# Start of a two-layer mixer trunk: squares folded on VectorE, the first modulation group taken k tile by k tile, lambda moved behind the conditioning row

## The chip, the cores and the metric

The kernel runs on one core of a Trainium2 chip, as one program. The metric is the device time of one execution in microseconds; the time of a kernel is the median of its runs. TensorE, VectorE, ScalarE and GpSimd each work through their own instruction queue in order, SyncE issues nearly all the transfers.

## The reference

256 tokens of width 2048 (16 tiles of 128 features) go through two layers. Each layer normalises the residual stream, modulates it with a scale and a shift made from a conditioning vector c, projects it once into the inputs of three mixers, and projects their gated outputs back.

```python
c_act = jax.nn.silu(c)
for l in range(DEPTH):
    shift, scale, gate = jnp.split(c_act @ w_ada[l] + b_ada[l], 3, axis=-1)
    h = rms_norm(x, norm_w[l]) * (1.0 + scale[:, None, :]) + shift[:, None, :]
    (gq, gk, gv, glr, gz, dq, dk, dv, da, db, dz, aq, ak, av, az) = jnp.split(h @ w_in[l], bounds, axis=-1)
    ...  # gated linear attention, gated DeltaNet
    lam = jnp.exp(jnp.sum(lv[0] * lv[1])) - jnp.exp(jnp.sum(lv[2] * lv[3])) + lam_init
    ...  # differential attention with lam
    y = jnp.concatenate([o_gla, o_gdn, o_diff], axis=-1) @ w_out[l]
    x = x + gate[:, None, :] * y
```

All is float32. `w_ada` is 2048 x 6144 and `w_in` about 2048 x 8200 for each layer, so the kernel streams some 270 MB of weights.

## The kernel before

The stream is kept with features on the partitions: `xt` is [128, 16 k tiles, 256 tokens]. A float32 product is made of three faster ones: `weights()` (L292) loads a chunk of 128 x 1024 into one of six buffers `raw`, ScalarE rounds it to `wh` (L300), VectorE takes the rest `wl = raw - wh` (L301), and TensorE sums wh·hh, wl·hh and wh·hl, where `hh` and `hl` are the same two parts of the modulated input. `wh` and `wl` have three buffers each.

The modulation's matrix-vector product is done on VectorE. `w_ada` comes in groups of eight pieces of 128 x 1024 (four output tiles, two halves of the sum each); `ada_group` (L313) multiplies each piece with the conditioning row `c_row` and accumulates (L325), and after the eighth piece four short ScalarE sums (L337) close scale and shift of two k tiles. Group g of the first eight gives scale (pieces 0 to 3) and shift (pieces 4 to 7) of k tiles 2g and 2g+1. All but the first group share the six buffers with the weights of the projection.

A layer's projection goes in passes over k, `STEPS` (L68): in layer 0 first blocks 18 to 27 (512 columns each, tokens on the output's partitions) over k tiles 0 and 1, then the same blocks over k tiles 2 and 3, and so on, so that it can start when one group of the modulation is there. Partial results are evacuated and added (`evac`, L427). While a pass runs, `advance` (L1087) traces the products of later groups and the modulation of k tiles between the chunks. Inside one block the order on TensorE is that of the trace, and a scheduler with a simulated timeline and priorities (`tc.high_priority`) writes the order of each engine's queue; `tc.manual_schedule` (`in_order`, L233) fixes the traced order for the engines that it names.

The start: SyncE loads the parameters `pt`, the conditioning row `c16`, the identity (first part of `ct`), x in four parts, and the first group's eight pieces `fr`. ScalarE squares x by parts, GpSimd folds the squares (L1066, L1068). In `rstd_rows` (L361) TensorE sums the squares over the partitions, GpSimd takes the power -1/2, ScalarE scales the identity by it twice (`dg`, L378), TensorE spreads it over the partitions, ScalarE copies that to `rb` in SBUF. `modulate` (L383) makes hn = rb · scale · x on VectorE (L388), `hh` on ScalarE (L389) and `hl` on VectorE (L390), for two k tiles in a call. The lambda of the differential attention is made at the very start (L272 to L282).

Of the kernel before, what the change touches and what calls it, by code (L numbers as in the profile page):

```python
# [18 lines left out]
P = 128  # L19
# [56 lines left out]
def in_chunks(layer, i):  # L76

    b0, b1, k0, k1 = STEPS[layer][i]
    out = []
    for b in range(b0, b1):  # L80
        for k in range(k0, k1):
            c = out[-1] if out else None
            if c is None or BLOCKS[c[-1][0]][0] != BLOCKS[b][0] or (k == k0 and BLOCKS[b][0] == "T") \
                    or _chunk_elems(c) + _width(b) > RAW:
                out.append([(b, k, k + 1)])
            elif c[-1][0] == b:
                c[-1] = (b, c[-1][1], k + 1)
            else:
                c.append((b, k, k + 1))
    return out  # L90
# [50 lines left out]
def hybrid_trunk(ctx: ExitStack, tc: tile.TileContext, x, cvec, pos, par, w_ada, w_in, w_out, w_lr, qkn, adt, cst, out):  # L141
# [91 lines left out]
    in_order = lambda: tc.manual_schedule(engines={mybir.EngineType.PE})  # L233
# [12 lines left out]
    SP.dma_start(ct[:, 0:128], cst[:, 0:128])  # L246
# [3 lines left out]
    first_raws = []  # L250
# [19 lines left out]
    nlam = const.tile([P, L], F32, name="nlam")  # L270
    ACT.activation(c16, c16, AF.Silu)
    pr = tiny("lp", 2 * L)  # L272
    lam = pcol("lam", 0, 4 * L).rearrange("p (m two) -> p m two", two=2)
    DVE.tensor_tensor(pr.rearrange("p (m o) -> p m o", o=1), lam[:, :, 0:1], lam[:, :, 1:2], ALU.mult)
    pb = bank("lam_ps", "a")
    mm(pb[:, 0:2 * L], ones, pr)
    el = tiny("el", 2 * L)
    ACT.activation(el, pb[:, 0:2 * L], AF.Exp)
    for l in range(L):
        init = 0.8 - 0.6 * math.exp(-0.3 * l)  # L280
        DVE.scalar_tensor_tensor(nlam[:, l:l + 1], el[:, 2 * l + 1:2 * l + 2], -init, el[:, 2 * l:2 * l + 1],
                                 ALU.add, ALU.subtract)  # L282
    for i in range(4):
        cb = bank("c_ps", "p")
        for j in range(4):
            mm(cb[:, 128 * j:128 * j + 128], ident[0:KT, 4 * i + j:4 * i + j + 1].broadcast_to([KT, P]), c16)
        (ACT.copy if i % 2 else DVE.tensor_copy)(c_row[:, 512 * i:512 * i + 512], cb)


    state = {"n": 0}  # L290

    def weights(src, n):  # L292

        raw = wraw.tile([P, RAW], F32, name="raw", tag="raw")[:, 0:n]
        wh = wsp.tile([P, RAW], F32R, name="wh", tag="wh")[:, 0:n]
        wl = wsp.tile([P, RAW], F32R, name="wl", tag="wl")[:, 0:n]
        with tc.high_priority(offset=AHEAD if state["n"] else 0):
            SP.dma_start(raw, src)
# [3 lines left out]
        state["n"] += 1  # L302
        return wh, wl

# [3 lines left out]
    DVE.tensor_scalar(pcol("b_ada", 0, 48 * L), pcol("b_ada", 0, 48 * L), 0.5, None, ALU.mult)  # L308
# [4 lines left out]
    def ada_group(l, g, raws=None):  # L313

        sums = tiny("ada_p", 8)
        for i in range(8):
            if raws is None:
                raw = wraw.tile([P, RAW], F32, name="rawa", tag="raw")[:, 0:1024]
                with tc.high_priority(offset=AHEAD):
                    SP.dma_start(raw, w_ada[l, g, i])  # L320
            else:
                raw = raws[i]
            cb = c_row[:, 1024 * (i % 2):1024 * (i % 2) + 1024]
            with tc.high_priority(offset=AHEAD):
                DVE.scalar_tensor_tensor(raw, raw, 1.0, cb, ALU.mult, ALU.mult, accum_out=sums[:, i:i + 1])  # L325
            if i < 7:
                yield
        for f in range(4):
            if g < 8:
                k = 2 * g + f % 2  # L330
                j = 0 if f < 2 else 1
            else:
                k = 4 * (g - 8) + f
                j = 2
            o, scale = ada[l][:, j, k:k + 1], pcol("norm", 16 * l + k) if j == 0 else 1.0
            bias = pcol("b_ada", 48 * l + (16, 0, 32)[j] + k)
            ACT.activation(tiny("ada_j", 2), sums[:, 2 * f:2 * f + 2], AF.Identity, bias=bias, scale=scale, accum_out=o)  # L337
        yield

    def ada_all():  # L340
        for l in range(L):
            for g in range(12):
                yield from ada_group(l, g, first_raws if l == 0 and g == 0 else None)

    ada_it = ada_all()
    ada_n = [0]
# [14 lines left out]
    def rstd_rows(sqs):  # L361
# [21 lines left out]
    def modulate(l, xt, rb, hh, hl, k):  # L383

        for i in range(k, k + 2):
            h = reg(i % 4, "hn")[:, 0:T]
            scale, shift = ada[l][:, 0, i:i + 1], ada[l][:, 1, i:i + 1]
            DVE.scalar_tensor_tensor(h, rb, scale, xt[:, i, :], ALU.mult, ALU.mult)  # L388
            ACT.activation(hh[:, i, :], h, AF.Identity, bias=shift)  # L389
            DVE.scalar_tensor_tensor(hl[:, i, :], h, shift, hh[:, i, :].bitcast(F32), ALU.add, ALU.subtract)  # L390


    in_off = [0]
# [25 lines left out]
    def project(l, group, hh, hl, o, after):  # L419
# [18 lines left out]
        for chunk in in_chunks(l, group):  # L438
            n = _chunk_elems(chunk)
            src = w_in[in_off[0]:in_off[0] + P * n].rearrange("(p n) -> p n", p=P)  # L440
            in_off[0] += P * n
            wh, wl = weights(src, n)
# [620 lines left out]
    for q in range(4):  # L1063
        p = sqx[:, 4 * q:4 * q + 4, :]
        ACT.activation(p, xt0[:, 4 * q:4 * q + 4, :], AF.Square)
# [6 lines left out]
    ada_to(ada_mark(0, 0))  # L1072

    for l in range(L):
# [12 lines left out]
        def advance(n, l=l, xt=xt, rb=rb, hh=hh, hl=hl, mod=mod):  # L1087

            while True:
                while mod[0] < KT and ada_n[0] >= ada_mark(l, mod[0] // 2):  # L1090
                    with tc.high_priority(offset=AHEAD):
                        modulate(l, xt, rb, hh, hl, mod[0])
# [5 lines left out]
        def block_done(b, done, last, l=l, o=o, g=g):  # L1098
            kind, name, i, _ = BLOCKS[b]
            lo, hi = span  # L1100
            if l == 0 and b == STEPS[0][0][0] and len(seen) == 0:
                seen.add("constants")
                load_constants()
# [55 lines left out]

        for i, (b0, b1, k0, k1) in enumerate(STEPS[l]):  # L1160
            advance(ada_mark(l, (k1 - 1) // 2))
# [126 lines left out]
```

## Time and profile before

| | us |
|---|---|
| median of 3 runs | 1101.14 |
| lowest and highest | 1100.52, 1104.81 |
| profiled execution, its own time | 1103.98 |
| its span, first to last instruction | 1102.2 |

| engine | busy us | share of the span |
|---|---|---|
| TensorE, matmul | 1047.0 | 95% |
| VectorE | 888.6 | 81% |
| ScalarE | 607.2 | 55% |
| GpSimd | 219.8 | 20% |

The profile is of one execution. Times in its rows are from the start of the span. A row of the timeline merges neighbours that are alike: "x8" are eight instructions, the time is from the first one's start to the last one's end. Instructions of one engine overlap a little, so a mean is longer than the distance of two starts. What stands in brackets is the idle time ahead and what ended it. PE is TensorE, PEld its weight loads, DVE VectorE, ACT ScalarE, POOL GpSimd, SP SyncE, and a name with q is the engine's queue of issues.

### The profile page before, as it was taken

The page shows a single profiled execution, that of the slowest core. Times are in us where ns is not written, and L with a number is a line of the kernel's source. Part 1 is how long each engine was busy: PE and PEld are TensorE (multiplying, and loading weights), DVE is VectorE, ACT ScalarE, POOL GpSimd, SP SyncE. Part 2 cuts the span into 40 slices and gives each one's busy share as a digit, 9 for nine tenths or more (in the row PEclk, how much of TensorE's full clock was granted, in tenths as well). Part 3 has the DMA queues.
Part 4 walks back from the last instruction along what each step waited for, and adds up shares of the span by engine and source line. Part 5 has one row for each costly group of instructions (what it writes and reads, how often), then busy time and mean ns, then how long its engine had stood idle before and what let it go on. Part 6 is the DMA issues. An engine that isn't in the chain of part 4 may idle for free.

```text
span 1102.2 us, 19699 instructions
## 1 busy us (share of the span) xinstructions
PE 1047.0 (95%) x7398; PEld 918.9 (83%) x7398; DVE 888.6 (81%) x1365; ACT 607.2 (55%) x1251; POOL 219.8 (20%) x284
## 2 busy tenths in 40 slices
PE   4999999999899989999979999999999999999998
PEld 3768888889898777898977877899989877889998
DVE  5899999998999886888687776677756776787874
ACT  4745544447765646466545555468444556557742
POOL 4000000040130841134210000024222144102400
PEclk9999999999999999999998999999999999999999
DMA  9888999999877545755588888796535645777472
GB/s 352 311 299 308 351 336 341 329 296 339 301 270 254 182 145 188 249 162 186 167 318 327 308 315 319 238 306 228 181 116 174 218 164 172 246 244 236 136 216 90
DMA packets 76799, 273.24 MB, mean 248 GB/s; under 512 B 8816, under 2 KB 9888, under 8 KB 76576
## 3 DMA queue, kind: packets, MB, share of 16 engines
q1 hardware_dynamic: 76704, 271.99, 71.7%
q8 instruction: 58, 0.95, 0.3%
q14 instruction: 37, 0.30, 0.1%
HBM read 267.76 MB, written 4.19 MB: 247 GB/s over the span
## 4 chain that ended last, share of the span: by engine, by line
PE 55%; DVE 18%; DMA 11%; issue 9%; ACT 5%; POOL 2%; SPq 0%; DVEq 0%; ACTq 0%; POOLq 0%
PE pt L180 20%; PE py L180 12%; PE pf L180 12%; DMA rawa<-in_w_ada 8%; DVE wl L301 6%; DVE rawa L325 5%; DMA raw<-in_w_in 2%; ACT wh L300 2%; PE Z_ps L180 1%; PE o_gdn L180 1%; DVE fr L325 1%; PE s_ps L180 1%; DVE aqk L436 1%; DVE z L436 1%; PE o_diff L180 1%
## 5 line engine op out<-in xcount | busy, mean ns | idle before, releaser
L300 ACT CAST wh<-raw 128x1024 fp32r<-128x1024 f32 (+1 forms) x312 | 320.0, 1028 | 272.9 <-PE pt L180 119.4
L301 DVE TENSOR_TENSOR wl<-raw,wh 128x1024 fp32r<-128x1024 f32 (+1 forms) x312 | 384.1, 1236 | 72.2 <-ACT wh L300 68.9
L180 PE MATMUL pt<-wl,hh 128*128 128x512 f32 (+1 forms) x768 | 293.5, 383 | 5.4 <-DVE wl L301 5.4
L180 PE MATMUL pt<-wh,hl 128*128 128x512 f32 (+1 forms) x768 | 291.7, 382 | 0.0
L325 DVE SCALAR_TENSOR_TENSOR rawa<-rawa,c_row 128x1024 f32<-128x1024 f32 x184 | 229.1, 1250 | 74.6 <-DMA rawa<-in_w_ada 74.3
L180 PE MATMUL pt<-wh,hh 128*128 128x512 f32 (+1 forms) x768 | 273.1, 383 | 8.5 <-ACT hh L389 4.3
L180 PEld LDWEIGHTS pt<-wh,hh 128*128 128x128 f32 x768 | 145.3, 191 | 40.6 <-ACT hh L389 5.7
L180 PEld LDWEIGHTS pt<-wl,hh 128*128 128x128 f32 x768 | 145.9, 190 | 38.3 <-DVE wl L301 10.4
L180 PEld LDWEIGHTS pt<-wh,hl 128*128 128x128 f32 x768 | 146.0, 190 | 28.7 <-issue 0.2
L180 PE MATMUL pf<-hh,wl 128*128 128x256 f32 x512 | 143.4, 283 | 3.5 <-DVE wl L301 3.5
L180 PE MATMUL pf<-hh,wh 128*128 128x256 f32 x512 | 144.3, 282 | 1.7 <-ACT wh L300 1.6
L180 PE MATMUL pf<-hl,wh 128*128 128x256 f32 x512 | 144.1, 282 | 0.0
L180 PE MATMUL py<-ogg,wh 128*128 128x256 f32 x512 | 101.1, 291 | 1.2 <-DVE xr L1183 0.6
L180 PEld LDWEIGHTS pf<-hh,wl 128*128 128x128 f32 x512 | 95.6, 188 | 6.0 <-DVE wl L301 4.2
L180 PEld LDWEIGHTS pf<-hh,wh 128*128 128x128 f32 x512 | 96.1, 188 | 3.1 <-ACT wh L300 1.8
L180 PEld LDWEIGHTS pf<-hl,wh 128*128 128x128 f32 x512 | 96.0, 188 | 1.5 <-issue 1.0
L180 PE MATMUL py<-odf,wh 128*128 128x256 f32 x512 | 91.4, 282 | 1.4 <-ACT odf L1028 1.0
L180 PEld LDWEIGHTS py<-ogg,wh 128*128 128x128 f32 x512 | 81.4, 190 | 3.2 <-DVE xr L1183 0.8
L180 PEld LDWEIGHTS py<-odf,wh 128*128 128x128 f32 x512 | 79.0, 190 | 2.5 <-ACT odf L1028 1.5
L337 ACT ACTIVATE ada_j<-ada_p,pt 128x2 f32<-128x2 f32 x96 | 31.1, 324 | 80.5 <-DVE rawa L325 72.8
L180 PE MATMUL py<-odf,wl 128*128 128x256 f32 x256 | 71.9, 282 | 1.4 <-DVE wl L301 1.3
L180 PE MATMUL py<-ogg,wl 128*128 128x256 f32 x256 | 72.7, 285 | 0.0
(277 smaller groups left out, 1335.9 us busy)
## 6 DMA issues: line engine op xcount, KB each, us to landing
raw<-in_w_in SPq DMA_DIRECT2D x224, 512.0 KB, 4.8
rawa<-in_w_ada SPq DMA_DIRECT2D x184, 512.0 KB, 4.8
raw<-in_w_out SPq DMA_DIRECT2D x64, 512.0 KB, 4.2
raw<-in_w_in SPq DMA_DIRECT2D x20, 402.0 KB, 4.4
fr<-in_w_ada SPq DMA_DIRECT2D x8, 512.0 KB, 10.6
xt<-in_x SPq DMA_DIRECT2D x4, 512.0 KB, 5.6
xr<-in_x SPq DMA_DIRECT2D x4, 512.0 KB, 8.2
xs<-xr SPq DMA_DIRECT2D x1, 2048.0 KB, 10.2
```

Of the source, the lines that this page charges most:

```text
L180: return PE.matmul(o, lhsT=lhsT, rhs=rhs, start=start, stop=stop, **kw)
L300: ACT.copy(wh, raw)
L301: DVE.tensor_tensor(wl, raw, wh.bitcast(F32), ALU.subtract)
L325: DVE.scalar_tensor_tensor(raw, raw, 1.0, cb, ALU.mult, ALU.mult, accum_out=sums[:, i:i + 1])
L337: ACT.activation(tiny("ada_j", 2), sums[:, 2 * f:2 * f + 2], AF.Identity, bias=bias, scale=scale, accum_out=o)
L436: DVE.tensor_tensor(d, src, d, ALU.add)
```

## The change

- Parameters and identity are loaded from ScalarE's queue instead of SyncE's; the first two chunks of `w_in` are loaded between the pieces of the first modulation group, and these pieces come in the order 0, 1, 4, 5, chunk, 2, 3, 6, 7, chunk.
- The folding of the squares goes from GpSimd to VectorE, with one more fold of 256 columns; `rstd_rows` sums one tile instead of two.
- All four copies of the conditioning row are VectorE's; the halving of `b_ada` is GpSimd's.
- `rstd_rows` spreads the statistics by one matmul for each token tile with the column as a broadcast stationary operand, and `rb` stays in PSUM. This holds for both layers.
- The lambda is traced behind the squares, on each engine behind the last instruction named.
- The first pass's first two chunks hold both first blocks for one k tile each, instead of one block for both k tiles.
- The first group's products, the casts and splits of these two chunks and the modulation of k tiles 0 and 1 are written out in order for VectorE and ScalarE. Only products 0, 1, 4 and 5 stand ahead of k tile 0.
- The rest of the constants is loaded behind the first pass's last chunk.
- The number of passes is the same.

The diff, cut to its core:

```diff
@@ in_chunks
+    if (layer, i) == (0, 0):
+        out = [[(b0, k, k + 1), (b0 + 1, k, k + 1)] for k in range(k0, k1)]
+        b0 += 2
@@ loads
-    SP.dma_start(pt, par)
     SP.dma_start(c16, cvec)
-    SP.dma_start(ct[:, 0:128], cst[:, 0:128])
+    ACT.dma_start(ct[:, 0:128], cst[:, 0:128])
+    ACT.dma_start(pt, par)
...
+    def load_first():
+        raw = wraw.tile([P, RAW], F32, name="raw", tag="raw")
+        SP.dma_start(raw, w_in[in_off[0]:in_off[0] + P * RAW].rearrange("(p n) -> p n", p=P))
+        in_off[0] += P * RAW
+        loaded.append(raw)
+
     for q in range(2):
         fr = t16("fr", [P, 4, 1024])
         for i in range(4):
-            SP.dma_start(fr[:, i, :], w_ada[0, 0, 4 * q + i])
-            first_raws.append(fr[:, i, :])
+            n = 4 * (i // 2) + 2 * q + i % 2
+            SP.dma_start(fr[:, i, :], w_ada[0, 0, n])
+            first_raws[n] = fr[:, i, :]
+        load_first()
@@ conditioning row (the lambda's lines go from here)
-        (ACT.copy if i % 2 else DVE.tensor_copy)(c_row[:, 512 * i:512 * i + 512], cb)
+        DVE.tensor_copy(c_row[:, 512 * i:512 * i + 512], cb)
...
-    DVE.tensor_scalar(pcol("b_ada", 0, 48 * L), pcol("b_ada", 0, 48 * L), 0.5, None, ALU.mult)
+    POOL.tensor_scalar(pcol("b_ada", 0, 48 * L), pcol("b_ada", 0, 48 * L), 0.5, None, ALU.mult)
@@ rstd_rows
-        dg = reg(8, "dg")[:, 0:T]
-        pb = bank("rstd_ps", "a")
-        rb = small.tile([P, T], F32, name="rb", tag="rb", bufs=1)
+        rb = bank("rstd_ps", "a")[:, 0:T]
...
             for t in range(2):
-                ACT.activation(dg[:, 128 * t:128 * t + 128], ident, AF.Copy, scale=r[:, t:t + 1])
-            mm(pb[:, 0:T], ones, dg)
-            ACT.copy(rb, pb[:, 0:T])
+                mm(rb[:, 128 * t:128 * t + 128], r[:, t:t + 1].broadcast_to([P, P]), ident)
@@ modulate: one k tile a call, and a hook between hh and hl
+        ACT.activation(hh[:, k, :], h, AF.Identity, bias=shift)
+        between()
+        DVE.scalar_tensor_tensor(hl[:, k, :], h, shift, hh[:, k, :].bitcast(F32), ALU.add, ALU.subtract)
@@ squares
-        POOL.tensor_tensor(p[:, 0:2, :], p[:, 0:2, :], p[:, 2:4, :], ALU.add)
-        if q > 0:
-            POOL.tensor_tensor(sqx[:, 0:2, :], sqx[:, 0:2, :], p[:, 0:2, :], ALU.add)
-    sq = [sqx[:, 0, :], sqx[:, 1, :]]
+            DVE.tensor_tensor(p[:, 0:2, :], p[:, 0:2, :], p[:, 2:4, :], ALU.add)
+            if q > 0:
+                DVE.tensor_tensor(sqx[:, 0:2, :], sqx[:, 0:2, :], p[:, 0:2, :], ALU.add)
+        last_fold = DVE.tensor_tensor(sqx[:, 0, :], sqx[:, 0, :], sqx[:, 1, :], ALU.add)
+    with tc.issue_after(last_fold.ins), tc.issue_after(squared.ins), tc.issue_after(spread.ins):
+        ...
+    sq = [sqx[:, 0, :]]
@@ layer 0, ahead of its first pass
+            def cast(i, a, z):
+                ACT.copy(first[i][0][:, a:z], loaded[i][:, a:z])
+
+            def split(i):
+                DVE.tensor_tensor(first[i][1], loaded[i], first[i][0].bitcast(F32), ALU.subtract)
+                done_first.append(first[i])
+
+            def meanwhile(i):
+                if i == 0:
+                    cast(0, 512, RAW)
+                    cast(1, 0, RAW)
+                    product(2)
+                split(i)
+
+            with tc.high_priority(offset=AHEAD), in_order(mybir.EngineType.DVE, mybir.EngineType.Activation):
+                with tc.issue_after(last_fold.ins):
+                    product(0)
+                product(1)
+                product(4)
+                cast(0, 0, 512)
+                product(5)
+                modulate(0, xt, rb, hh, hl, 0, lambda: meanwhile(0))
+                for n in (3, 6, 7):
+                    product(n)
+                modulate(0, xt, rb, hh, hl, 1, lambda: meanwhile(1))
...
+            if l == 0 and i == 1:
+                with tc.issue_after(last_dma[0].ins):
+                    load_constants()
```

`product(n)` is the accumulating VectorE product of piece n with the conditioning row; after an odd n it adds the ScalarE sum that closes the column n // 2.

## Rows read from the trace of the kernel before

**Rows 1.** Windows: stretch, length, busy us of the engines (instructions), granted clock, transfers
```profile
0.00:56.90 56.90, 40.64 (x165) 33.43 (x166) 39.81 (x63) 34.76 (x65) 11.89 (x14) 1.00 0.89 331
56.90:91.80 34.90, 31.37 (x134) 23.51 (x133) 34.76 (x54) 14.68 (x24) 0.00 (x0) 1.00 0.81 276
...
200.00:230.00 30.00, 30.00 (x130) 24.20 (x129) 30.00 (x49) 12.98 (x20) 1.04 (x3) 1.00 0.94 319
```

**Rows 2.** The chain that ended last, 0 to 110 us: start, length, what
```profile
4.00 8.87 DMA fr<-in_w_ada
...
15.01 9.82 DVE fr L325 x14
...
27.11 27.13 PE pt L180 x108
...
57.58 1.22 DVE wl L301
...
91.83 5.36 DMA rawa<-in_w_ada
```

**Rows 3.** Timeline of SyncE's queue: issues of loads
```profile
0.72 0.39 SPq L237 DMA_DIRECT2D pt<-in_par  x1
...
2.09 1.86 SPq L249 DMA_DIRECT2D xt<-in_x  x4
...
15.45 0.33 SPq L320 DMA_DIRECT2D rawa<-in_w_ada  x1
...
23.12 0.33 SPq L491 DMA_DIRECT2D posi<-in_pos  x1
```

**Rows 4.** Timeline of the start: conditioning row, squares, folds, products
```profile
3.63 7.16 PE L180 MATMUL c_ps<-c,ct 16*128 16x128 f32 x32
...
11.60 1.06 ACT L1065 ACTIVATE sqx<-xt 128x1024 f32<-128x1024 f32 x1 [1.42 <-DMA xt<-in_x]
...
13.96 4.45 POOL L1068 TENSOR_TENSOR sqx<-sqx 128x512 f32<-128x512 f32 x2
...
15.01 2.27 DVE L325 SCALAR_TENSOR_TENSOR fr<-fr,c_row 128x1024 f32<-128x1024 f32 x1
...
20.56 1.21 DVE L325 SCALAR_TENSOR_TENSOR fr<-fr,c_row 128x1024 f32<-128x1024 f32 x1
```

**Rows 5.** Groups of VectorE instructions by line and shape: busy us, mean ns | idle before
```profile
L1183 DVE SCALAR_TENSOR_TENSOR xr<-py,ada,xr 128x256 f32<-128x256 f32 x96 | 45.2, 477 | 23.6 <-PE py L180 19.9 <-DMA xr<-xs 3.4
...
L325 DVE SCALAR_TENSOR_TENSOR fr<-fr,c_row 128x1024 f32<-128x1024 f32 x8 | 12.2, 1587 | 3.2 <-DMA fr<-in_w_ada 3.2
...
L925 DVE TENSOR_TENSOR scr<-scr 128x512 f32<-128x512 f32 x16 | 10.9, 684 | 0.3
...
L388 DVE SCALAR_TENSOR_TENSOR hn<-rb,ada,xt 128x256 f32<-128x256 f32 x16 | 7.5, 475 | 0.0
```

**Rows 6.** Timeline of the start: row statistics to the first projection matmuls
```profile
21.38 0.97 POOL L359 TENSOR_TENSOR rs<-ms,mhalf 128x2 f32<-128x2 f32 x1 [2.98 <-ACT ms L375]
...
23.13 1.22 PE L180 MATMUL rstd_ps<-dg,ones 128*128 128x256 f32 x2 [2.81 <-ACT dg L378]
...
27.11 1.22 PE L180 MATMUL pt<-wh,hh 128*128 128x512 f32 x2 [2.75 <-ACT hh L389]
...
30.26 0.63 PE L180 MATMUL pt<-wl,hh 128*128 128x512 f32 x1
...
30.96 0.39 PE L180 MATMUL pt<-wl,hh 128*128 128x512 f32 x1
```

**Rows 7.** Windows: two microseconds of the second layer's first matmuls, columns as in rows 1
```profile
582.00:584.00 2.00, 2.00 (x5) 1.61 (x6) 2.00 (x6) 1.11 (x3) 0.00 (x0) 0.50 0.94 401
```

**Rows 8.** Waits of VectorE, 28 to 60 us: total, times, longest
```profile
DVE wl L301 <- ACT wh L300: 5.8, 8, 2.0
```

**Rows 9.** Timeline of the second layer's start: ScalarE's part of the row statistics
```profile
578.48 0.69 ACT L378 ACTIVATE dg<-ct,rs 128x128 f32<-128x128 f32 x2 [0.82 <-POOL rs L359]
...
580.48 0.37 ACT L380 COPY rb<-rstd_ps 128x256 f32<-128x256 f32 x1 [0.75 <-PE rstd_ps L180]
```

More of the change, by code (lines that the diff above doesn't have):

```diff
@@ L231, in mm @@
             self.first = False
-    in_order = lambda: tc.manual_schedule(engines={mybir.EngineType.PE})
+    in_order = lambda *e: tc.manual_schedule(engines=set(e or (mybir.EngineType.PE,)))
     pt = const.tile([P, NPAR], F32, name="pt")
-    SP.dma_start(pt, par)
     def pcol(name, i, n=1):
@@ L269, in hybrid_trunk @@
     junk_n = [0]
-    nlam = const.tile([P, L], F32, name="nlam")
     ACT.activation(c16, c16, AF.Silu)
[L272 to L282, printed above, removed]
     for i in range(4):
@@ L311, in hybrid_trunk, with ada_product, ada_finish, ada_group @@
                                  ALU.add, ALU.mult)
-    def ada_group(l, g, raws=None):
+    def ada_product(raw, i, sums):
+        cb = c_row[:, 1024 * (i % 2):1024 * (i % 2) + 1024]
+        with tc.high_priority(offset=AHEAD):
+            DVE.scalar_tensor_tensor(raw, raw, 1.0, cb, ALU.mult, ALU.mult, accum_out=sums[:, i:i + 1])
+    def ada_finish(l, g, sums, f):
+        if g < 8:
+            k = 2 * g + f % 2
+            j = 0 if f < 2 else 1
+        else:
+            k = 4 * (g - 8) + f
+            j = 2
+        o, scale = ada[l][:, j, k:k + 1], pcol("norm", 16 * l + k) if j == 0 else 1.0
+        bias = pcol("b_ada", 48 * l + (16, 0, 32)[j] + k)
+        ACT.activation(tiny("ada_j", 2), sums[:, 2 * f:2 * f + 2], AF.Identity, bias=bias, scale=scale, accum_out=o)
+    def ada_group(l, g):
         sums = tiny("ada_p", 8)
         for i in range(8):
[L317 to L323, printed above, removed]
+            raw = wraw.tile([P, RAW], F32, name="rawa", tag="raw")[:, 0:1024]
             with tc.high_priority(offset=AHEAD):
-                DVE.scalar_tensor_tensor(raw, raw, 1.0, cb, ALU.mult, ALU.mult, accum_out=sums[:, i:i + 1])
+                SP.dma_start(raw, w_ada[l, g, i])
+            ada_product(raw, i, sums)
             if i < 7:
@@ L328, in ada_group @@
         for f in range(4):
[L329 to L337, printed above, removed]
+            ada_finish(l, g, sums, f)
         yield
@@ L342, in ada_all @@
             for g in range(12):
-                yield from ada_group(l, g, first_raws if l == 0 and g == 0 else None)
+                if (l, g) != (0, 0):
+                    yield from ada_group(l, g)
     ada_it = ada_all()
-    ada_n = [0]
+    ada_n = [8]
     def ada_to(n):
@@ L377, in rstd_rows, with modulate @@
             for t in range(2):
[L378 to L393 removed]
+                mm(rb[:, 128 * t:128 * t + 128], r[:, t:t + 1].broadcast_to([P, P]), ident)
+        return rb
+    def modulate(l, xt, rb, hh, hl, k, between=lambda: None):
+        h = reg(k % 4, "hn")[:, 0:T]
+        scale, shift = ada[l][:, 0, k:k + 1], ada[l][:, 1, k:k + 1]
+        DVE.scalar_tensor_tensor(h, rb, scale, xt[:, k, :], ALU.mult, ALU.mult)
+        ACT.activation(hh[:, k, :], h, AF.Identity, bias=shift)
+        between()
+        DVE.scalar_tensor_tensor(hl[:, k, :], h, shift, hh[:, k, :].bitcast(F32), ALU.add, ALU.subtract)
     class Out:
@@ L439, in project @@
             n = _chunk_elems(chunk)
-            src = w_in[in_off[0]:in_off[0] + P * n].rearrange("(p n) -> p n", p=P)
-            in_off[0] += P * n
-            wh, wl = weights(src, n)
+            if done_first:
+                wh, wl = done_first.pop(0)
+            else:
+                src = w_in[in_off[0]:in_off[0] + P * n].rearrange("(p n) -> p n", p=P)
+                in_off[0] += P * n
+                wh, wl = weights(src, n)
             off, polled = 0, 0
@@ L1091, in advance @@
                     with tc.high_priority(offset=AHEAD):
-                        modulate(l, xt, rb, hh, hl, mod[0])
+                        for k in range(2):
+                            modulate(l, xt, rb, hh, hl, mod[0] + k)
                     mod[0] += 2
@@ L1158, in after, with product @@
             yield from gen
+        if l == 0:
+            sums = tiny("ada_p", 8)
+            def product(n):
+                ada_product(first_raws[n], n, sums)
+                if n % 2 == 1:
+                    ada_finish(0, 0, sums, n // 2)
+            first = [[wsp.tile([P, RAW], F32R, name=n, tag=n) for n in ("wh", "wl")] for _ in range(2)]
+            def cast(i, a, z):
[20 more added lines that the diff above has]
+                modulate(0, xt, rb, hh, hl, 1, lambda: meanwhile(1))
+            mod[0] = 2
         for i, (b0, b1, k0, k1) in enumerate(STEPS[l]):
+            if l == 0 and i == 1:
+                with tc.issue_after(last_dma[0].ins):
+                    load_constants()
             advance(ada_mark(l, (k1 - 1) // 2))
```

35 lines of the change are left out of this document (22 added, 13 removed).

## The prediction, made before the changed kernel ran

> **What bounds the kernel now.** I read the windows first, to see which engine is full in which stretch, then the chain that ended last over the first 110 us, then the timeline of the start, since nearly all of the edit lies ahead of the first projection matmul. In the first 56.9 us TensorE is busy 40.64 us, from 56.9 to 91.8 VectorE is busy 34.76 of 34.9 us and TensorE only 31.37, and by 200 to 230 both are full [rows 1]. So the first pass is paced by TensorE once it has started, the second by VectorE, and later stretches by both. The chain says the same: a transfer of the first modulation weights up to 12.87, VectorE's products of them up to 24.83, TensorE alone from 27.11 to 54.24, VectorE from 57.58, then a weight transfer of 5.36 us [rows 2]. A start that comes earlier is therefore worth what it brings forward on TensorE at the end of pass one, less what VectorE can't follow.
>
> The pass is 10 blocks x 2 k tiles x 2 token tiles x 3 = 120 matmuls. TensorE runs them 0.231 us apart when all is well (130 in 30.00 us) [rows 1].
>
> **The start, part by part.**
>
> *Loads.* Two issues ahead of x leave SyncE's queue (parameters and identity go to ScalarE's). The first load was issued at 0.72 and x at 2.09, with three loads ahead [rows 3]; with one ahead, x is issued near 1.17, 0.9 us earlier. The 186 KB that left still share the engines, at most 0.5 us at 350 to 415 KB/us. I take 0.8 (bounds 0.4 to 0.9). ScalarE's two extra issues, 0.4 us each, fall where it waited for the conditioning row. Later issues on SyncE are released by landings: seven from 15.45 to 23.12, 1.28 us apart [rows 3]; that is the landing pitch of 512 KB. So modulation weights 0, 1, 4, 5 land at 12.1, 13.4, 14.6, 15.9, the first w_in chunk at 17.2, weights 2, 3, 6, 7 at 18.5 to 22.3, and the second w_in chunk at 23.6.
>
> *Folding on VectorE.* The last square began at 11.60, when its x had landed, and took 1.06 [rows 4]; now 10.8 to 11.9. Behind it stand two 128x512 adds and one 128x256. The nearest VectorE row has 0.68 for 128x512 in SBUF [rows 5]; with the half-size one at 0.4 that is 1.7 us: products may start at 13.6, against 12.99 now, so 0.6 later. The earlier folds hide in waits for x. All four copies of the conditioning row on VectorE hide too: the spreading matmuls end at 10.79 [rows 4], a little earlier without the lambda matmul ahead.
>
> *What the folding gives back.* While GpSimd folded (four and a half us from 13.96 alone), a product took 2.27 us; alone it takes 1.21, and the next starts 1.15 after it [rows 4]. All eight cost 12.2 us [rows 5]; alone 8 x 1.15 = 9.2. So 3.0 us come back on VectorE, less the 0.6: by 2.4 us VectorE is ahead in work.
>
> *k tile by k tile.* Only products 0, 1, 4, 5 stand ahead of k tile 0: 13.6 + 4 x 1.15 = 18.2. The row statistics are hidden: sums end near 14.6, the GpSimd power takes 0.97 and the spreading matmuls 1.22 [rows 6], so 17.2 without the scaled diagonals and the copy. Then `hn` 0.45, the closing ScalarE sum 0.45 beside it, `hh` 0.45: the first projection matmul at 19.2 instead of 27.11 [rows 6]. That is not yet the gain, for k tile 1 has a queue of its own on VectorE, in a fixed order: `hn` 0.4, product 2 1.15, `wl` 1.15, `hl` 0.45, products 3, 6, 7 3.45. From 18.2 this gives 24.9 (weights 7 landed at 22.3, so it doesn't wait); the ScalarE sum closes at 25.3 and `hh` of tile 1 is there at 25.9. Here the wait added is ScalarE's: the cast of the second chunk stands ahead of the closing sums, and whoever waits for those is `hn` of tile 1. It lands at 23.6 and ends at 24.65, so 0.6 us in hand. `wl` and `hl` of tile 1 end at 26.5 and 26.9.
>
> *TensorE.* Now its first nine matmuls come 0.43 us apart (27.11 to 30.96, 0.63 long, then 0.39) [rows 6]; in the second layer five such matmuls fill 2.00 us of a stretch whose granted clock is 0.50 [rows 7]. [...] The first 24 matmuls are therefore issued by 30.96 + 15 x 0.231 = 34.4, and 96 x 0.231 = 22.2 bring 56.6, where the windows have the pass ending. After the change twelve are done on tile 0 from 19.2, at 0.43 by 24.4, in time that was idle. In the trace the change of level came 3.9 us after the first matmul [rows 6]; I take the clock as up when tile 1 comes. The other twelve run from 25.9 at 0.231: 28.7. That is 34.4 - 28.7 = 5.7 us of lead. The four PSUM banks of the two blocks finish together; the first is evacuated 0.6 us after its last matmul, near 28, so it costs nothing.
>
> *Can VectorE follow?* It waited 5.8 us for casts between 28 and 60, eight times [rows 8]. Its own lead is 2.4 us, and waits that a TensorE further ahead removes give the rest. If none went, 2.4 us would be left at the start of the VectorE-bound stretch; if enough did, 5.7. I take 5.0, as these casts waited for buffers that TensorE frees. The 512 KB of constants now load behind the pass's last weights, which takes 1.28 us of transfers from it.
>
> *Lambda.* An exponential with its table load (1.3 us) moves behind the fourth square. ScalarE has nothing else until the sums near 14.6, and spreading the row statistics waits for its bank until about 13.4: no cost; uncovered it would be 1.5 us.
>
> *Second layer.* The scaled diagonals (0.69) and the copy (0.37) leave the path there [rows 9], with their hops some 1.15 us. VectorE is then in a product, so I take 0.9 (0.3 to 1.2).
>
> *Statistics in PSUM.* 32 `hn` now read PSUM. The same operation of the same size with a PSUM operand (`xr`) takes 477 ns, without (`hn`) 475 [rows 5]: nothing. [...] The bank is held until the sixteenth modulation, which is traced ahead of the tasks that use that pair of banks.
>
> **Sum.** 5.0 + 0.9 = 5.9 us. The profiled run took 1103.98 (span 1102.2, 1.8 around it); it becomes 1098.1, span 1096.3. The median is 2.8 lower than that run: 1101.14 - 5.9 = 1095.2.
>
> **Rivals.**
> 1. *The clock is not up when tile 1 comes.* TensorE idles from about 24.4 to 25.9, right when the clock should have risen. If the twelve of tile 1 run at 0.43 for nine of them, 24 are done at 30.5, the lead is 3.9 and, with 0.9, the gain 4.8: 1096.3. For it: the second layer's slow rows after a short idle [rows 7]; against: 5.2 us of work before a gap of 1.5. [...]
> 2. *VectorE doesn't follow.* Its waits for casts stay, its lead is 2.4, and the full stretch behind passes on no more: 2.4 + 0.9 = 3.3, 1097.8. For it: 34.76 of 34.9 busy [rows 1]. Lower bound of the same: a late x (0.4 us) and a second chunk landing a microsecond late, 2.0 in all, 1099.1.
> 3. *Slower.* Starting earlier meets transfers that can't: product after product in pass two finds its weights not landed. Such a wait stands in the chain at 91.83 with 5.36 us [rows 2]. The six buffers are refilled only as they are freed, and VectorE, in order, holds `wl` behind the waiting product, for which TensorE waits. One more such wait leaves 0.5 of the gain; from the second on it is slower: 5.9 - 10.7 = -4.8, 1106. Against it: TensorE is full later although transfers are.
>
> **How the numbers follow.** About 0.5% (5.5 us, 1095.6) is what a measurement of this kernel can tell from no change. Forecast 0.47, rival 1 0.22, rival 2 0.21, rival 3 0.10. The forecast's own range is 1093.5 to 1096.5, and some three fourths of it is faster by more than 0.5%, 0.36; adding a share of rival 1 that has the full second-layer gain and less wait gives 0.42. Of rival 3 about half passes 1106.6: 0.06. The rest, 0.52, is within 0.5%. The range reaches from 1093.0 (5.7 + 1.2, and a little run to run) to 1100.0 (rival 2's lower bound).
>
> **What would show it.** First projection matmul near 19.2, `hh` of tile 1 near 25.9, the eight first products about 1.2 us each with no GpSimd work beside them, TensorE's gap between the two tiles under 2 us, and 0.39 us matmuls from the second on. The second pass should start near 51.6 instead of 56.6, with VectorE waiting less than 5.8 us before it. In the second layer `hn` follows the spreading matmuls directly. Wrong would be: product 0 later than 14, cast of the second chunk ending after 25.3, 0.63 us matmuls behind 26, or a new wait of VectorE for a weight transfer in the second pass.

## The result, and the profile of the changed kernel

The changed kernel is slower: median 1120.12 us of four runs (1113.79 to 1121.68) against 1102.97 of four runs of the kernel before (1100.52 to 1107.12). The recorded ratio is 1.0127, 95% interval [1.0079, 1.0174]; the two medians alone give 1.0155. The forecast was 1095.2, with 0.06 for slower. The profiled execution is the fastest of the four, 1113.79, with a span of 1112.0, 9.8 longer than before's.

The start came out almost as worked out. Timeline of the changed kernel's start (VectorE, TensorE, ScalarE); it answers to [rows 4, 6]:

```profile
13.74 1.22 DVE L318 SCALAR_TENSOR_TENSOR fr<-fr,c_row 128x1024 f32<-128x1024 f32 x1
...
18.46 0.48 DVE L390 SCALAR_TENSOR_TENSOR hn<-rstd_ps,ada,xt 128x256 f32<-128x256 f32 x1
...
19.59 2.07 PE L184 MATMUL pt<-wh,hh 128*128 128x512 f32 x4 [1.63 <-ACT hh L391]
...
25.63 0.51 ACT L391 ACTIVATE hh<-hn,ada 128x256 fp32r<-128x256 f32 x1
...
26.19 1.20 PE L184 MATMUL pt<-wh,hh 128*128 128x512 f32 x4 [1.40 <-ACT hh L391]
...
29.44 0.50 PE L184 MATMUL pt<-wh,hh 128*128 128x512 f32 x1
```

Products start at 13.74 (worked out: 13.6), the first projection matmul at 19.59 (19.2), `hh` of k tile 1 ends at 26.14 (25.9). The wait between the two tiles is 1.40 and four matmuls behind it take 1.20 us together, against 2.07 for the first four at 19.59, so they run at the faster pace, and the 24th projection matmul is done near 29.4 (28.7).

To see what became of it, I number the projection matmuls (`pt`, `pf`, `py`; 5376 in all, 120 of them the first pass, 1920 the input projection of layer 0, then 192, 192 and 384 for the outputs of GLA, DeltaNet and differential attention) and set the n-th start after against the n-th before:

```
n                0   24  119  400 1200 1600 1919 2111 | 2112 2304 2687 2688 3700 4000 5375
before, us    27.1 34.5 56.6  110  267  330  436  478 |  479  516  571  582  775  841 1099
after - before -7.5 -5.0 -4.8 -4.7 -5.2 -5.6 -5.6 -5.6 | +7.9 +4.7 +7.7 +7.1 +6.8 +9.8 +9.8
```

By this count the lead of 5 us reaches matmul 2111 undiminished. Between 2111 and 2112 it turns to a lag of 7.9: 13.5 us at one place, the boundary between GLA's output projection and DeltaNet's. The lag is 4.7 at 2304, 7.7 at 2687 and 9.8 at 4000, and stays there.

Windows cut at the same matmuls (0, 1920, 2304, 2688), columns as in [rows 1]; first before, then after:

```profile
0.00:437.70 437.70, 406.56 (x2734) 347.50 (x2734) 393.36 (x596) 242.84 (x502) 83.03 (x90) 0.99 0.82 287
437.70:515.70 78.00, 75.83 (x582) 70.17 (x581) 67.55 (x142) 48.35 (x121) 21.49 (x44) 0.98 0.64 211
515.70:582.00 66.30, 55.39 (x419) 52.55 (x419) 51.61 (x74) 30.39 (x62) 16.39 (x22) 0.91 0.68 242
```

```profile
0.00:432.70 432.70, 407.25 (x2700) 345.26 (x2701) 394.94 (x603) 238.61 (x494) 76.44 (x85) 0.98 0.83 292
432.70:520.30 87.60, 79.87 (x611) 73.17 (x609) 68.24 (x139) 50.09 (x121) 16.12 (x35) 0.96 0.54 175
520.30:589.00 68.70, 56.20 (x424) 53.45 (x424) 52.87 (x77) 30.48 (x63) 20.53 (x32) 0.91 0.66 236
```

The first stretch is 5.0 shorter, but TensorE has done 34 instructions less in it (2700 against 2734): DeltaNet work that before was behind it by then is still to come. The second is 9.6 longer: 7.73 us of TensorE idle instead of 2.17, 29 instructions more, a lower clock. So part of the 13.5 is postponed work, which the count of projection matmuls had flattered, and 5.6 are new idle time.

A count of all of TensorE's instructions (7398 in either kernel) shows how much. When the changed kernel starts projection matmul 2111 it has done 2989 of them, before had done 3045; at matmul 2112 it is 3049 and 3047. Set by the n-th instruction of any kind, the two kernels are level, within 0.5 us, from the 2750th (441.6 us in before) to the 2950th (467.1), and at the 3050th (480.2) the changed one is 7.3 us behind. So the 5 us of the start are gone by 442 us, and the boundary costs some 7 us more.

What TensorE does at the boundary. Timeline of the changed kernel, TensorE:

```profile
473.20 1.08 PE L184 MATMUL o_gdn<-vn,E 64*64 64x128 f32 x8
474.21 1.09 PE L184 MATMUL o_gdn<-S_gdn,fm 128*64 128x128 f32 x8
...
477.26 1.90 PE L184 MATMUL s_ps<-aqk 128*128 128x128 f32 x12
...
480.70 0.33 PE L188 MATMUL oT_ps<-ct,z 128*128 128x128 f32 x1 [1.42 <-ACT scr L956]
484.48 0.48 PE L188 MATMUL aT_ps<-ct,scr 128*128 128x128 f32 x1 [3.45 <-DVE scr L970]
...
486.95 1.42 PE L184 MATMUL py<-ogg,wh 128*128 128x256 f32 x4
```

The last `o_gdn` and the attention's first scores stand behind the last matmul of GLA's output, with no projection matmul left to run beside them. TensorE's queue then holds a transpose of the attention (`aT_ps`) ahead of the first `py`, and it waits 1.42 and 3.45 us for the softmax. Without that transpose little would change: the first `py` needs the DeltaNet's gated output `z`, which GpSimd ends at 484.02, half a microsecond before the transpose starts. Timeline of the changed kernel, GpSimd:

```profile
482.76 1.26 POOL L1023 TENSOR_TENSOR z<-z,on_gdn 128x512 f32<-128x512 f32 x1
```

In before the same work stands inside GLA's output projection. Timeline of before, TensorE:

```profile
466.67 1.09 PE L180 MATMUL o_gdn<-S_gdn,fm 128*64 128x128 f32 x8
467.69 0.71 PE L180 MATMUL s_ps<-aqk 128*128 128x128 f32 x4
468.16 0.36 PE L180 MATMUL py<-ogg,wh 128*128 128x256 f32 x1
```

Its `z` is done at 476.25, with projection matmuls running meanwhile (GpSimd):

```profile
474.96 1.29 POOL L1018 TENSOR_TENSOR z<-z,on_gdn 128x512 f32<-128x512 f32 x1
```

In TensorE's compiled queue the DeltaNet chain of layer 0 has moved, counted by the projection matmuls ahead of a step, from its first transposes (CT) over its sums of squares (ssq) and products with the state (wS) to its outputs (o_gdn): CT 1612 before, 1636 after; ssq 1841 and 1889; first wS 1920 and 1980; last o_gdn 2041 and 2112. The traced order of the last pass is the same: where it is forced there (experiments 5 and 6), CT is at 1722 and ssq at 1866 in either kernel. The scheduler, which writes the queues from its own simulated timeline, put the steps later.

The 5 us of the start go before the boundary. Waits of TensorE in the changed kernel, 390 to 450 us, where before has one of 3.4 and none of the second kind over 0.2:

```profile
PE Y_ps L184 <- DVE Um L798: 3.9, 1, 3.9
PE py L184 <- DVE z L438: 2.3, 2, 2.1
```

Behind some waits the clock is low, too. Windows of the changed kernel behind two waits of TensorE (the 3.9 us for the DeltaNet's `Um`, and the 1.42 and 3.45 above):

```profile
392.00:402.00 10.00, 8.07 (x45) 5.71 (x46) 9.37 (x16) 1.76 (x3) 1.60 (x1) 0.54 0.41 147
...
482.00:489.00 7.00, 4.52 (x19) 4.26 (x20) 3.49 (x8) 4.83 (x15) 2.32 (x4) 0.54 0.06 22
```

The granted clock is 0.54 in both. By windows of 2 us it reads 1.00 from 386 to 392, 0.72 to 394, 0.50 from 394 to 402, 0.72 to 404 and 1.00 from 404 to 410; projection matmuls of 512 columns start 0.43 us apart from 400 to 402, and 0.23 apart ahead of the wait. In the second it reads 0.50 from 482 to 486, of which 2.5 us are still the wait itself. In before the wait of 3.4 us ended at 395.5, and the clock read 0.62 from there to 400 and 1.00 from 400 to 410. So between 390 and 450 the changed kernel loses, by an estimate from these figures, 0.5 and 2.1 us of wait and some 3 of clock: about the 5 us. Over the whole run TensorE's busy time grows by 8.1 us (1047.0 to 1055.1) and its idle time by only 1.7 (55.2 to 56.9), as the start's idle time shrank. The mean granted clock falls from 0.988 to 0.982: with 0.50 as the lower level, some 2 x 0.012 x 1102 = 26 us at it before, 2 x 0.018 x 1112 = 40 after. By this estimate half of the 14 more, about 7 us, explains most of the 8.1.

### The profile page after: what moved, and what is told of

It is laid out like the page before. It is cut to its first block, busy times and chain, and to the rows that moved or that the text cites. A ratio compares the mean times of both kernels' runs of the same rounds, so it can differ in the third digit from the quotient of the medians.

```text
span 1112.0 us, 19696 instructions
## 1 busy us (share of the span) xinstructions
PE 1055.1 (95%) x7398; PEld 922.6 (83%) x7398; DVE 892.2 (80%) x1373; ACT 605.7 (54%) x1244; POOL 205.6 (18%) x279
## 4 chain that ended last, share of the span: by engine, by line
PE 49%; DVE 23%; DMA 11%; issue 9%; ACT 3%; POOL 3%; DVEq 0%; ACTq 0%
PE pt L184 19%; PE py L184 13%; DMA rawa<-in_w_ada 10%; DVE rawa L318 8%; PE pf L184 8%; DVE wl L302 7%; ACT wh L301 1%; PE o_gdn L184 1%; DVE on_gdn L662 1%; DVE z L438 1%; DMA raw<-in_w_in 1%; DVE aqk L438 1%; PE Y_ps L184 1%; PE ropeT_ps L188 1%; PE Z_ps L184 1%
## 5 line engine op out<-in xcount | busy, mean ns | idle before, releaser
L301 ACT CAST wh<-raw 128x1024 fp32r<-128x1024 f32 (+2 forms) x310 | 318.3, 1029 | 299.1 <-PE pt L184 135.3
L302 DVE TENSOR_TENSOR wl<-raw,wh 128x1024 fp32r<-128x1024 f32 (+2 forms) x310 | 382.2, 1238 | 69.7 <-ACT wh L301 68.4
## 6 DMA issues: line engine op xcount, KB each, us to landing
xs<-xr SPq DMA_DIRECT2D x1, 2048.0 KB, 10.3
```

## The experiments

Theory A: the start gains what was forecast, and the loss is the late place of the DeltaNet chain. Rival B: an early start itself brings a loss in the middle. Further theories are in the expectations.

**1 and 2. Two versions whose queues have the old places.** The lambda's product on VectorE, and the folds back on GpSimd; each of them puts the first wS at 1920 again (and the last o_gdn at 2009, before 2041).

```diff
-        POOL.tensor_tensor(pr.rearrange(...), lam[:, :, 0:1], lam[:, :, 1:2], ALU.mult)
+        DVE.tensor_tensor(pr.rearrange(...), lam[:, :, 0:1], lam[:, :, 1:2], ALU.mult)
```

> The changed kernel with one edit: the 128x4 lambda product is VectorE's instead of GpSimd's. In the compiled queues this puts the gated DeltaNet's steps of layer 0 back where they stood before (its first state matmul behind 1920 projection matmuls instead of 1980, its last output behind 2009 instead of 2112). Theory A (the loss is the later place of that chain in the queues; the start gains 5 us as predicted): no stall at the end of the first output projection, 14 us less than the changed kernel, about 0.993 to 0.997 of the kernel before. Theory B (the loss comes from what the new start does on the chip: statistics in PSUM, transfers shifted against the passes, a lead that later stages can't use): unchanged, about 1.01.

```diff
-            DVE.tensor_tensor(p[:, 0:2, :], p[:, 0:2, :], p[:, 2:4, :], ALU.add)
+            POOL.tensor_tensor(p[:, 0:2, :], p[:, 0:2, :], p[:, 2:4, :], ALU.add)
             if q > 0:
-                DVE.tensor_tensor(sqx[:, 0:2, :], sqx[:, 0:2, :], p[:, 0:2, :], ALU.add)
+                POOL.tensor_tensor(sqx[:, 0:2, :], sqx[:, 0:2, :], p[:, 0:2, :], ALU.add)
```

> The changed kernel with the folds of the squares back on GpSimd (the last fold of 256 columns stays VectorE's). The compiled queues have the chain of layer 0 back in its old place, the rest of the new start stays. Theory A: 1 to 4 us faster than the kernel before (5 us of lead less up to 3 us of slower products beside the folds), 0.996 to 0.999. Theory B, if the folds aren't the culprit: about 1.01.

Both missed what theory A had: 1115.78, ratio 1.0105 [1.0085, 1.0125], and 1115.18, 1.010 [1.0083, 1.0116]. The jump at 2112 is gone in both (lag 11.7 to 11.1, and no jump in the other), but they lose elsewhere, first at the start. Timeline of the run with the lambda on VectorE, TensorE and VectorE:

```profile
17.36 0.59 PE L184 MATMUL lam_ps<-lp,ones 128*128 128x4 f32 x2 [6.87 <-DVE lp L1080]
17.81 0.99 PE L184 MATMUL ss<-ones,sqx 128*128 128x1 f32 x4
...
22.43 2.08 PE L184 MATMUL pt<-wh,hh 128*128 128x512 f32 x4 [1.18 <-ACT hh L391]
```

The lambda's matmul stands ahead of the sums of the squares and waits for VectorE; `hn` comes 2.8 us later, and products of the next group have slipped in front of `hn` and `hl` of k tile 1, so that the 24th matmul is 3.1 us behind before, not 5.0 ahead. With the folds on GpSimd the first matmul is at 22.07 and the lag 2.1. Some 12 us more go between matmuls 1919 and 2000, of which 4 come back by 2111; there TensorE waits 4.6 (4.1) us for VectorE's evacuation `z`; in the run with folds on GpSimd the ten microseconds behind it have a granted clock of 0.50. So these two show that the jump goes with the places; they don't show a gain, and their times are what rival B had.

**3. The chain later, the start old.** Two of the chain's planned pauses are longer in the kernel before, by 2.5 and 1.0 us in layer 0 (the text on record has 1.8 and 0.9).

```diff
-            yield YW[12]
+            yield YW[12] + (2.5 if l == 0 else 0.0)
...
-            yield YW[13]
+            yield YW[13] + (1.0 if l == 0 else 0.0)
```

> The kernel before, its start untouched; in layer 0 the gated DeltaNet's solve steps are traced 1.8 us (Y) and 0.9 us (Z) later on the planner's clock, which puts the chain's first state matmul behind 1957 projection matmuls instead of 1920 and its last output behind 2108 instead of 2041, nearly as in the changed kernel. Theory A: projection matmuls run out before the chain is done; 6 to 14 us slower, 1.005 to 1.013. Theory B: the start is the old one, so no change, 1.000.

1127.34, ratio 1.0211 [1.0182, 1.0241], more than the 1.005 to 1.013 of theory A. The lag goes from 10.5 at matmul 2111 to 22.0 at 2112: 11.5 us at the same boundary, with no edit at the start. Waits of TensorE in that run, 400 to 600 us (total, times, longest):

```profile
PE oT_ps L184 <- POOL z L1018: 10.8, 2, 9.0
```

The `z` waited for is the DeltaNet's gated output, as above. A chain that ends late is enough for such a jump, with the old start. The rest was lost before it and, some 5 us, in layer 1.

**4. The fold alone.**

```diff
-        POOL.tensor_tensor(p[:, 0:2, :], p[:, 0:2, :], p[:, 2:4, :], ALU.add)
+        DVE.tensor_tensor(p[:, 0:2, :], p[:, 0:2, :], p[:, 2:4, :], ALU.add)
         if q > 0:
-            POOL.tensor_tensor(sqx[:, 0:2, :], sqx[:, 0:2, :], p[:, 0:2, :], ALU.add)
+            DVE.tensor_tensor(sqx[:, 0:2, :], sqx[:, 0:2, :], p[:, 0:2, :], ALU.add)
```

> The kernel before with the folds alone on VectorE; the chain's place in the queues is the old one. Theory A and the prediction's working: products cost 1.2 us each instead of up to 2.3, so the first projection matmul comes 1 to 2.5 us earlier than 27.1, ratio 0.997 to 0.999. Theory B with the folds as culprit: slower, about 1.01.

1100.44, ratio 0.9968 [0.9947, 0.9988], the places as before; theory A had 0.997 to 0.999. It is the one version whose median lies below both kernels'. Its trace doesn't show where the gain comes from: the execution profiled is one of its slower ones (1104.26), 2.4 us ahead at the first matmul, 0.6 at the 24th and level with before at the end.

**5 and 6. The same places in both kernels.** TensorE's queue is written in the traced order for the last pass of layer 0, in the changed kernel and in the one before.

```diff
-            project(l, i, hh, hl, o, block_done)
+            if l == 0 and i >= 6:
+                with in_order():
+                    project(l, i, hh, hl, o, block_done)
+            else:
+                project(l, i, hh, hl, o, block_done)
```

> The changed kernel with TensorE's queue written in the traced order for the last pass of layer 0 (k tiles 12 to 15); VectorE's and ScalarE's queues at the start are those of the changed kernel. In TensorE's queue the DeltaNet's CT now stands behind 1722 projection matmuls, its ssq behind 1866, its first wS behind 1920 and its last o_gdn behind 2009 (changed kernel 1636, 1889, 1980, 2112; kernel before 1612, 1841, 1920, 2041). Theory A, the loss is only the DeltaNet's late place behind the start's lead: no jump of more than 3 us between projection matmuls 2111 and 2112, the 24th matmul still about 5 us earlier than before, the end 4 to 7 us earlier than the kernel before with the same order forced on it, which puts it at 0.990 to 1.002 of before. Rival B, the early start itself brings a loss in the middle (transfers, VectorE, the clock) wherever the chain stands: at or above 1.008, and no faster than the kernel before with forced order. Rival C, the order's effect is a matter of VectorE's and GpSimd's queues and not TensorE's: the jump stays above 8 us.

> The kernel before with the same forced order in the last pass of layer 0: CT behind 1722 matmuls, ssq 1866, first wS 1920, last o_gdn 2027. It is the base for the run beside it. Theory A: the chain ends where it ended before (2041), so the time is within 0.5% of before, 0.995 to 1.006; a wait of TensorE inside the last pass may cost some us, since the traced order puts CT 110 matmuls later and the rest closer together. Rivals B and C say the same of this one.

1122.66, ratio 1.0151 [1.0121, 1.018], and 1121.37, 1.0134 [1.0103, 1.0165]. Both miss theory A's numbers: the traced order puts the chain's steps close together and TensorE waits for them in the projection, in before as well (5.3 and 5.1 us for the chain's first `C` at matmul 1722; either loses 8.7 us against before between matmuls 1600 and 1800). From matmul 2111 to 2112 it is 0.1 us in the changed kernel, 14.3 without the forced order, so rival C falls. Rival B's condition, above 1.008 and no faster than the kernel before in this order, is met. Changed kernel less kernel before, both in this order, in the two profiled executions:

```
n        0    24   1200   1600   1800   2112   5375
us    -7.8  -5.3   -5.1   -2.8   -2.7   -2.0   -2.5
```

The lead of 5 us is down to 2.8 at matmul 1600, ahead of the wait for `C`, and 2.5 reach the end. That is of these two executions; by the medians the changed kernel is 1.3 us slower, and the intervals of the two ratios overlap, so no gain is shown. Here too the lead of TensorE alone was not worth its length.

**7. The order fixed in the output projection only.**

```diff
-        out_project(0, ot["gla"], add, pace)
+        if l == 0:
+            with in_order():
+                out_project(0, ot["gla"], add, pace)
+        else:
+            out_project(0, ot["gla"], add, pace)
```

> The changed kernel with the traced order only in the first 192 matmuls of the output projection (1920 to 2111): the DeltaNet's chain up to ssq stands as late as in the changed kernel (1889), its first wS is forced to 1944 and its last o_gdn to 2028, the attention's first s_ps to 2100. Theory A: the place is early, but the operands come as late as before it, so TensorE waits inside the output projection instead of at its end; the jump at 2112 falls below 4 us, and the loss shows between 1920 and 2112 instead; in all between the changed kernel and the fixed order, 1.000 to 1.010. Rival C: no better than the changed kernel, 1.012 or more.

1109.87, ratio 1.0035 [1.0013, 1.0057]: 10.3 us less than the changed kernel's median, as theory A has it (1.000 to 1.010). The step from 2111 to 2112 is 1.9 us instead of 14.3, so the late place made that step. But the start's 5 us don't show in this time either: 8.7 us are lost against the changed kernel between 1920 and 2000, where the chain stands now and its operands come as late as ever.

**8. The old statistics in the changed kernel.** `rstd_rows` as before the change.

```diff
-                mm(rb[:, 128 * t:128 * t + 128], r[:, t:t + 1].broadcast_to([P, P]), ident)
+                ACT.activation(dg[:, 128 * t:128 * t + 128], ident, AF.Copy, scale=r[:, t:t + 1])
+            mm(pb[:, 0:T], ones, dg)
+            ACT.copy(rb, pb[:, 0:T])
```

> The changed kernel with the row statistics made and held as before (scaled diagonals, copy to SBUF); its TensorE queue keeps the late places (wS 1980, last o_gdn 2112). Theory A: the same jump of 11 to 16 us between matmuls 2111 and 2112, and in the second layer the 0.9 us of the prediction given back, the start about 0.7 us later: 1.011 to 1.018. [...]

1123.38, ratio 1.0158 [1.0127, 1.0189]. The places are the late ones and the step from 2111 to 2112 is the same, 14.3 us; the time is in the range of theory A. The first matmul is 1.1 us later and the 24th 2.3. The `hn` read SBUF again and take 477 and 480 ns, so the statistics in PSUM weren't what made the changed kernel slower.

**9 and 10. A shorter chain.** One doubling level of layer 0's solve is left out in both kernels.

```diff
+            if n == 2 and l == 0:
+                continue
             C = reg(8, "C")
```

> The changed kernel with one of the five doubling levels of layer 0's DeltaNet solve left out (the second; its products, its copy and its two subtractions are not made, so the solve is of less). The chain then has its last o_gdn behind 2009 projection matmuls in TensorE's queue instead of 2112, the first wS behind 1920 instead of 1980. Theory A, the loss is the chain's late end at the boundary of the two output projections: the jump of 13.5 us between matmuls 2111 and 2112 falls to 3 us or less, and the time is 0.990 to 1.000 of before; the start's lead at the 24th matmul, about 5 us, is unchanged. Rival B, the early start loses its time in the middle whatever the chain does: 1.006 or more. With the same edit in the kernel before beside it, theory A has this one 3 to 8 us faster than that one, rival B slower.

> The kernel before with the same doubling level left out. Its chain ends behind 2013 matmuls instead of 2041. Theory A: before lost little at that boundary (0.7 us between matmuls 2111 and 2112), so little is to be had, 0.994 to 1.002. Rival B says the same.

Changed kernel 1105.07, ratio 1.0007 [0.9993, 1.002], just above theory A's 0.990 to 1.000; kernel before 1117.28, 1.0119 [1.0103, 1.0135], a miss. Either does 96 instructions of TensorE less than the full kernels, so it is the pair that compares. The jump at 2112 is gone: lags of the changed kernel's fastest execution (1101.62, the one profiled) against the full kernel before are -2.8 at 2111, -3.4 at 2112, -2.4 at the end. Timeline of the changed kernel with the short chain, TensorE, where the last `o_gdn` stands among projection matmuls again:

```profile
459.73 1.09 PE L184 MATMUL o_gdn<-S_gdn,fm 128*64 128x128 f32 x8
460.74 0.71 PE L184 MATMUL s_ps<-aqk 128*128 128x128 f32 x4
461.21 0.36 PE L184 MATMUL py<-ogg,wl 128*128 128x256 f32 x1
```

The changed kernel is 12.2 us faster than the one before with the same edit, where theory A had 3 to 8 and rival B the opposite sign. Not all of that is the start's, though, for the kernel before lost 13 us in a way that neither theory foresaw. VectorE and TensorE of that run, behind matmul 1920:

```profile
441.15 1.23 DVE L325 SCALAR_TENSOR_TENSOR rawa<-rawa,c_row 128x1024 f32<-128x1024 f32 x1 [3.07 <-DMA rawa<-in_w_ada]
...
442.30 0.69 DVE L436 TENSOR_TENSOR z<-pt,z 128x512 f32<-128x512 f32 x1
...
443.04 0.58 PE L180 MATMUL py<-ogg,wh 128*128 128x256 f32 x1 [4.53 <-DVE z L436]
```

A product waits 3.07 us for its weights, the evacuation `z` stands behind it on VectorE, and TensorE waits 4.53 for `z`. A chain that is shorter can therefore make the kernel slower: what counts is what stands in each queue when the input projection ends.

**11. VectorE's wait for GpSimd taken away.** In GpSimd's queue the chain's third `C` product has moved behind GLA's statistics, right ahead of GLA's second normalised output `mix`; in before it ran some 10 us ahead of `mix`, with the fourth between them. Timelines of GpSimd, first before, then after:

```profile
380.28 2.27 POOL L783 TENSOR_TENSOR C<-Lm,ct 128x512 f32<-128x512 f32 x1
...
391.91 1.03 POOL L644 TENSOR_TENSOR mix<-scr,ss_gla 128x512 f32<-128x512 f32 x1
```

```profile
389.20 1.28 POOL L788 TENSOR_TENSOR C<-Lm,ct 128x512 f32<-128x512 f32 x1
390.44 1.04 POOL L649 TENSOR_TENSOR mix<-scr,ss_gla 128x512 f32<-128x512 f32 x1
```

The rotary products on VectorE overwrite what `mix` reads and wait for it, and the chain's `Um` stands behind them. Waits of VectorE in the changed kernel, 330 to 440 us (in before the two are 2.2 and 1.9):

```profile
DVE scr L928 <- POOL mix L649: 5.6, 1, 5.6
DVE scr L926 <- POOL mix L649: 3.2, 1, 3.2
```

With the order of experiment 7, the rotary products get other scratch tiles:

```diff
-                A, B = scr[:, hf], scr[:, 2 + hf]
+                A, B = scr[:, 4 + hf], scr[:, 6 + hf]
```

> The changed kernel with the traced order in the first 192 matmuls of the output projection (the run that reached 1.0035) and the rotary products of the differential attention in four other scratch tiles, so that VectorE's products no longer wait for GpSimd's GLA output (3.2 and 5.6 us in the changed kernel). Places of the chain in TensorE's queue are the same or a little later (ssq 1897, first wS 1944, last o_gdn 2028). If VectorE's wait made the chain late, the chain's ssq comes 4 to 6 us earlier and the time falls to 0.994 to 1.000. If the places in TensorE's queue make it late, which I hold likelier since TensorE ran through there, ssq moves by less than 2 us and the time stays at 1.001 to 1.006.

1108.49, ratio 1.0042 [1.0026, 1.0058]. The two waits are gone. Both branches were half wrong: the chain's ssq does come 5.9 us earlier than in experiment 7 (417.0 against 422.9), so VectorE's wait had made it late, and TensorE is 11.4 us ahead of before at matmul 1919; but by 2000 it is 2.6 behind. It now waits 3.2 us for GLA's gated output (`ogg`), which is not ready at that time. The time stays; where the rest of that lead went isn't shown.

**12. The two parts that leave the places alone**, fold and statistics, in the kernel before (the edit of 4 and the reverse of 8).

> The kernel before with two parts of the change that leave its queue order in the middle: the squares folded on VectorE, and the row statistics spread by a broadcast column and kept in PSUM. Places as before (last o_gdn 2041). Theory A: folding gave 0.9968; the statistics add the 0.9 us of the second layer and up to 0.7 us at the start: 0.993 to 0.998. If reading PSUM cost VectorE time, 0.997 to 1.000.

1104.85, ratio 1.0003 [0.9982, 1.0025], its runs from 1097.0 to 1110.0: a miss, though it holds the edit of 4 (0.9968). Its trace is 1.3 ahead at matmul 24 and 2.0 at 3200, then loses 5 in layer 1 between 3700 and 4000, where the clock read 0.90 from 810 to 845 us (1.00 from 774 to 845 in the run of 4). I can't say from it what the statistics are worth.

## Why the prediction was wrong

- *The start* held: 5.7 of lead worked out, 5.0 measured at matmul 24 [rows 6]. TensorE's 24th matmul was 0.7 late. (VectorE's steps from 18.2 add up to 24.8, not 24.9, which changes nothing.)
- *Can VectorE follow?* It did: 5.0 was taken for the start of pass two, 4.8 was measured. VectorE's waits for casts up to there fell from 5.8 us [rows 8] to 3.0. Rivals 1 and 2, which concerned this, didn't occur.
- *The failed step is the sum.* "5.0 + 0.9" carries the lead at pass two through to the end of the kernel. The runs show that it doesn't get there: by all of TensorE's instructions it was gone by 442 us, and the boundary of two output projections, in a stretch that the prediction never looked at, cost some 7 us more. None of the signs of being wrong that it named came, for all lie in the first 90 us. Three things were missed. First, a lead of TensorE is kept only while its work needs nothing else: at the end of the input projection it needs the ends of three mixers, whose steps go through VectorE, ScalarE and GpSimd in turn (the 3.9 and 2.1 us above), and with the order forced at most 2.5 of 5 came through (5, 6). Second, the queues of the middle are not those of before: the chain's end moved from 2041 to 2112, from inside a stretch of projection matmuls to its end, where nothing hides it (3, 7, 9). Third, the clock can be low behind a wait, here 0.54 over ten microseconds from 392, against 1.00 ahead of it.
- *Rival 3* had the sign and not the place. Products of pass two did not wait more. Its mechanism, a product that waits for a transfer with VectorE's work for TensorE behind it, occurs in the kernel before with the short chain, at matmul 1920 (3.07 us of VectorE's wait, 4.53 of TensorE's).
- *Second layer.* 0.9 was taken; from the end of the power to `hn` it is 1.88 us instead of 2.45, 0.6 less, and the power itself took 1.55 instead of 0.71 in this execution, so nothing was left.
- *Statistics in PSUM* held: 32 `hn` take 476 and 478 ns, 475 before [rows 5].

What stays open: why the scheduler moves the chain. In the kernels run with the start of the changed one and the full chain, the places up to ssq are late (1889 to 1897, but where the order was forced there), and in the two whose first matmul came at 22 us they are those of before, which suggests that its own timeline takes TensorE's lead into account and the other engines' lack of it. That is argued, not shown. Also, the trace explains 9.8 us; the median of the runs lost 17, and the executions in between have no trace. The nearest is experiment 8, with the same late places and a span of 1122.0, whose further loss is spread over several stretches.

## What to carry to other kernels

A lead won at the start is worth, at the end, what the next join lets through: list the joins behind the edit (a stage for which several engines' chains must end) and ask of each what ends last there, before adding a saving to the sum. Where a scheduler writes the queues, compare the compiled queues of the whole kernel, above all how many matmuls stand ahead of each step of a chain and what is left to hide its end; an edit at the start can move work some 400 us later. Order that is forced by hand is no cure by itself: it cost 1.3% in the kernel before.

## What the runs showed of the hardware that was not expected

Behind some waits of TensorE the clock was low, and with that a wait cost up to about twice its length, by the estimate below: 0.54 in 392 to 402 behind 3.9 us in the changed kernel, 0.50 for ten microseconds behind 4.1 us in the run with the folds on GpSimd. It needn't: behind 4.4 us in the changed kernel with the short chain, the low level lasted 3.5 us (0.52). Windows of that run:

```profile
391.50:395.00 3.50, 3.31 (x19) 2.78 (x20) 3.50 (x8) 1.17 (x2) 1.16 (x1) 0.52 0.35 119
395.00:402.00 7.00, 7.00 (x60) 5.62 (x59) 7.00 (x10) 2.82 (x4) 3.38 (x4) 1.00 0.39 112
```

By an estimate from these rows (the wait and half of the low time behind it, as matmuls of 512 columns started 0.43 us apart at 0.50 and 0.23 apart at 1.00) the price was 1.4 to 2.2 times the wait. Over the whole changed kernel, of the 9.8 us lost, 8.1 are longer busy time of TensorE and 1.7 idle time.
